# First gate made inside the attention, modulation spread over the MLP, fc2 sums in fc1's PSUM banks, relu squared on ScalarE

## The chip, the cores and the metric

The kernel runs on one core of a Trainium2 chip. The metric is the device time of one execution in microseconds; the time before is the median of three runs.

## The reference, cut to what matters

Two trunk layers work on 128 context tokens and 512 latent tokens, 1024 wide, all in float32. A conditioning vector (one for the context, one for the latents) gives six modulation vectors per layer: shift, scale and gate for the attention, shift, scale and gate for the MLP.

```python
def modulation(cond, w_ada_l, b_ada_l):
    m = (silu(cond) @ w_ada_l + b_ada_l)[:, None, :]
    return split(m, 6)          # vectors 0 to 5
def mlp_residual(x, shift, scale, gate, g, w1, w2):
    h = rms_norm(x, g) * (1 + scale) + shift
    return x + gate * (square(relu(h @ w1)) @ w2)
for l in range(2):
    h = rms_norm(y, norm_mix_g[l]) * (1 + m[1]) + m[0]
    o = diff_attend(h) if l == 0 else neighbourhood_attend(h)
    y = y + m[2] * (o @ w_o[l])          # m[2]: the first gate
    y = mlp_residual(y, m[3], m[4], m[5], norm_mlp_g[l], w_fc1[l], w_fc2[l])
```

`w_fc1` is 1024 by 4096, `w_fc2` 4096 by 1024, `w_ada` 1024 by 6144 per layer.

## The kernel before, in words

The 640 tokens are five tiles of 128. Every float32 product is three matmuls on a high and a low part (`hi`, `lo`): `split` makes the high part with a ScalarE copy and the low part with a subtraction on VectorE (or GpSimd). Weights come in column chunks of 384, 256 and 384 (`CHUNKS`); `load_block` loads one into three `raw` buffers and splits it into one of two `w` buffers. All loads are issued by SyncE (SP), whose queue runs in order.

Layer 0's attention goes over 8 groups of heads times 5 token tiles in slots; `SLOT` and `START` are orders written out by hand (`pin` holds PE, VectorE, ScalarE and GpSimd to them). A digit stands for so many projection matmuls; `fma` is one step of `ada_cols`, which makes modulation vectors 4 and 3 of layer 0: two steps of four small matmuls (`ada_products`) for 256 columns, a ScalarE copy, and a step that turns the row into columns (`to_cols`). The steps run in slots with `n < self.FMA`, and what is left is run at once where the tail begins (`begin`). The tail is the output projection `out_proj`; it runs in the last slots at `TAIL` steps per unit, and makes the first gate (vector 2) itself: `gate_steps` calls `ada_rows` three times, each with three loads into the `raw` buffers, eight program matmuls, a copy, and two matmuls that spread the row over 128 partitions. In layer 1 the gate is read from the DRAM tensor `gate_d`.

The MLP goes over `D_FF` in four quarters: `fc1` (8 units of 128 hidden columns, 48 matmuls each, sums in the two double banks tagged `s`) and then `fc2` (three chunks times five token tiles, 24 matmuls each, sums in the two banks tagged `g`). The hidden columns `u` are kept as `hi` and `lo` in nine buffers. `add_gated` multiplies a sum by the gate into a buffer tagged `B` (three of them, shared with `relu`) and adds it to `x`.

In layer 0's MLP `ada_fma` runs beside this (`fill`): 112 units, each a load of 128 rows of `w_ada` (`fraw`, `ahead` + 1 buffers), a multiply-add on VectorE (L427), a scaled copy on ScalarE (L429) and an addition on GpSimd (L430). They make the second gate of layer 0 (16 units) and the six vectors of layer 1. Eight units make one half vector; `finish` (four steps into the next) turns it with 8 transposes (L394) or sums it with matmuls against ones (L405). There is one step at the start, one a unit, and one at the end: 114. Three steps run after each unit of `fc1`, one after each tile of `fc2`. Instructions of the MLP are ordered by the framework's list scheduler, not by hand. The last chunk of the last quarter is `last_chunk`, which also makes the next norm.

Of the kernel before, what the change touches and what calls it, by code (L numbers as in the profile page):

```python
# [15 lines left out]
P = 128  # L16
# [12 lines left out]
LAMBDA_INIT = 0.2  # L29


class Kernel:
# [274 lines left out]
    def ada_rows(self, l, c0, n):  # L307

        nc = self.nc
        view = self.I["w_ada"][l].rearrange("(k p) n -> p k n", p=P)  # L310
        cuts = ((0, 3), (3, 6), (6, 8))
        raws = [self.load_raw(view[:, k0:k1, c0 : c0 + n]) for k0, k1 in cuts]
        pr = self.psum_g(n)
        yield pr
        raws = [raw[:, k] for (k0, k1), raw in zip(cuts, raws) for k in range(k1 - k0)]
        for h in range(2):
            self.ada_products(pr, raws[4 * h : 4 * h + 4], h)
            for _ in range(6):
                yield

# [21 lines left out]
    def ada_cols(self, jobs, pool, ahead):  # L342

        nc = self.nc
        units = [(*job, c0, kh) for job in jobs for c0 in range(0, D, 256) for kh in range(2)]
        raws = []

        def load():
            if len(raws) < len(units):
                l, vec, c0, kh = units[len(raws)]  # L350
                raw = pool.tile([P, 4, 256], F32, tag="fraw", bufs=ahead, name="fraw")
                src = self.I["w_ada"][l, kh * 512 : kh * 512 + 512, vec * D + c0 : vec * D + c0 + 256]
                nc.sync.dma_start(raw, src.rearrange("(k p) n -> p k n", p=P))
                raws.append(raw)

        for _ in range(ahead):
            load()
        yield
        for i, (l, vec, c0, kh) in enumerate(units):
            if kh == 0:  # L360
                pr = self.psum_t().rearrange("p a b -> p (a b)")[:, 0:256]
            self.ada_products(pr, [raws[i][:, k] for k in range(4)], kh)
            load()
            if kh == 1:
                rows = pool.tile([P, 256], F32, tag="ftmp", bufs=2, name="rows")
                nc.scalar.activation(rows, pr, AF.Copy)
                yield
                self.to_cols(l, vec, c0, 256, rows)
            yield

    def ada_fma(self, jobs, pool, ahead, gate=None, share=False, wait=()):
# [15 lines left out]
        def finish(l, vec, h, acc):  # L387
# [19 lines left out]
            for j in range(4):  # L407
                dst = self.gate_d[vec // 3, j // 2 : j // 2 + 1, h * 512 + j % 2 * 256 : h * 512 + j % 2 * 256 + 256]
                nc.sync.dma_start(dst, row[32 * j : 32 * j + 1])
            if l == 0 and h == 1:  # L410
                self.load_gate(1, gate)
# [27 lines left out]
    def load_gate(self, which, gate):  # L439
        for ci in range(2):  # L440
            self.nc.sync.dma_start(gate[ci], self.gate_d[which, ci : ci + 1].partition_broadcast(P))
# [537 lines left out]
    def gate_steps(self, l, c, gate):  # L979
# [3 lines left out]
        if l:  # L983
            for ci in range(2):
                nc.sync.dma_start(gate[ci][:, :n], self.gate_d[0, ci : ci + 1, c0 : c0 + n].partition_broadcast(P))
            yield
            return
        for ci in range(2):
            nc.sync.dma_start(gate[ci][:, :n], self.I["b_ada"][l : l + 1, 2 * D + c0 : 2 * D + c0 + n].partition_broadcast(P))
        rows = self.ada_rows(l, 2 * D + c0, n)  # L990
        pr = next(rows)
        yield
        for _ in rows:
            yield
        row = self.tmp()[:, :n]
        nc.scalar.activation(row, pr, AF.Copy)
        for ci in range(2):
            pb = self.psum_g(n)
            nc.tensor.matmul(pb, self.sel[:, 2 + ci * P : 2 + (ci + 1) * P], row, start=True, stop=True)
            nc.vector.tensor_tensor(gate[ci][:, :n], pb, gate[ci][:, :n], ALU.add)  # L1000
            for _ in range(4):
                yield
# [66 lines left out]
    def fc1(self, l, q, up, fill, w=None, begin=None):  # L1069
# [17 lines left out]
        for c0, n in CHUNKS:  # L1087
# [9 lines left out]
            for i, cs in enumerate(cols):  # L1097
# [9 lines left out]
                nc.scalar.activation(u[:, 0], r, AF.Square)  # L1107
                nc.vector.tensor_tensor(r, r, r, ALU.mult)  # L1108
                nc.vector.tensor_tensor(u[:, 1], r, u[:, 0].bitcast(F32), ALU.subtract)  # L1109
                us.append(u)  # L1110
                for _ in range(3):
                    next(fill, None)
        return us

    def fc2(self, l, q, us, gate, fill, chunks=CHUNKS):
        act = lambda kt, t: (us[kt][:, 0, t * P : (t + 1) * P], us[kt][:, 1, t * P : (t + 1) * P])
        for c0, n in chunks:
            ww = self.load_block(self.I["w_fc2"][l], q * D, c0, n)
# [26 lines left out]
    FMA = 0  # L1145
# [12 lines left out]
    TAIL = 3.75, 2.75  # L1158
    WLO = (0, 1, 2), (0, 1, 2)
    KB, VB, QTB, EB, ATB, UB = 2, (15, 17), 6, 4, (2, 3), 9  # L1160

    def run(self):
# [3 lines left out]
        with ExitStack() as ctx:  # L1166
# [5 lines left out]
            self.gate_d = self.dram.tile([2, 2, D], F32, name="gate_d")  # L1172
# [20 lines left out]
            for l in range(2):  # L1193
# [53 lines left out]
                def early():  # L1247
# [6 lines left out]
                    if l:  # L1254
                        self.load_gate(1, gate)
                        return iter(())
# [3 lines left out]
                    cmF.append(self.ada_fma(jobs, fpool, 2, gate))  # L1260
# [3 lines left out]
                f = iter(()) if l else cmF[1]  # L1264
# [4 lines left out]
                for _ in f:  # L1269
# [80 lines left out]
```

## Time and profile before

| | |
|---|---|
| median of three runs (lowest to highest) | 1797.42 us (1795.93 to 1798.04) |
| profiled execution: time, span | 1797.07 us, 1795.3 us |
| PE, PEld busy | 1708.6 us (95%), 1624.1 us (90%) |
| VectorE (DVE), ScalarE (ACT), GpSimd (POOL) busy | 1133.0 (63%), 836.1 (47%), 527.8 us (29%) |
| mean granted clock of TensorE | 0.982 |
| layer 0's MLP from its first unconditional stretch of `fc1` to its last `fc1` | 472.97 to 860.65 us |
| the same stretch of layer 1's MLP | 1347.90 to 1678.50 us |

Busy times of PE are modelled at their ends, so that "PE busy" tells less than the time from one stretch's start to the next. The two stretches in the last rows hold the same matmuls of `fc1` and `fc2`; layer 1's has no `ada_fma` beside it. A wait is put down to the engine and line that ended it.

### The profile page before, as it was taken

How to read it: one execution, taken by the hardware profiler on the slowest of the kernel's cores; microseconds unless marked ns; L12 is line 12 of the kernel's file. 1: busy time of each engine (PE TensorE's matmuls, PEld its weight loads, DVE VectorE, ACT ScalarE, POOL GpSimd, SP SyncE). 2: the span in 40 equal slices, each digit the busy share in tenths (PEclk: the TensorE clock that was granted, in tenths of full speed). 3: DMA queues.
4: the chain of work that ended last, by engine and by line, in shares of the span. 5: the costliest groups of instructions: out<-in, count | busy, mean ns of one | idle time of the engine just before them, and what ended most of it. 6: DMA issues, size and time to landing. Idle time of an engine off the chain costs nothing.

```text
span 1795.3 us, 30528 instructions
## 1 busy us (share of the span) xinstructions
PE 1708.6 (95%) x11353; PEld 1624.1 (90%) x11353; DVE 1133.0 (63%) x2269; ACT 836.1 (47%) x2426; POOL 527.8 (29%) x575
## 2 busy tenths in 40 slices
PE   7899999998988989979999999999989999999999
PEld 4699999787878989969999899998889999999999
DVE  5588888765888798786345666667673433434343
ACT  4477777643653353441225777777353222132220
POOL 1334444124554353340004654543350000000000
PEclk8899999999999999989999999999999999999999
DMA  9832453432355355343212433332232222222231
GB/s 297 246 92 58 107 135 99 138 115 82 110 161 185 115 168 173 111 136 118 71 63 76 120 97 85 93 104 88 64 109 68 71 72 82 66 88 71 65 98 50
DMA packets 209397, 195.10 MB, mean 109 GB/s; under 512 B 39447, under 2 KB 193087, under 8 KB 209247
## 3 DMA queue, kind: packets, MB, share of 16 engines
q1 hardware_dynamic: 209246, 193.14, 36.2%
q8 instruction: 89, 1.46, 0.3%
q14 instruction: 62, 0.50, 0.1%
HBM read 182.95 MB, written 16.44 MB: 111 GB/s over the span
## 4 chain that ended last, share of the span: by engine, by line
PE 69%; DVE 10%; ACT 8%; DMA 5%; issue 5%; POOL 2%; SPq 1%; DVEq 0%; POOLq 0%; ACTq 0%
PE ps_g L146 40%; PE pz L1081 16%; DMA fraw<-in_w_ada 3%; DVE acc L427 3%; PE ps_t L712 2%; PE ps_t L886 2%; PE ps_t L741 1%; PE ps_s L736 1%; PE ps_s L735 1%; DVE w L42 1%; PE ps_t L875 1%; DVE relu L1108 1%; ACT E L785 1%; ACT sq L631 1%; POOL rs L118 1%
## 5 line engine op out<-in xcount | busy, mean ns | idle before, releaser
L146 PE MATMUL ps_g<-w,hT 128*128 128x384 f32 (+1 forms) x2544 | 538.8, 347 | 12.4 <-ACT hT L41 4.8
L146 PE MATMUL ps_g<-w,u 128*128 128x384 f32 (+1 forms) x2880 | 463.2, 321 | 27.6 <-DVE u L1109 17.3
L146 PEld LDWEIGHTS ps_g<-w,u 128*128 128x128 f32 x2880 | 452.9, 190 | 34.5 <-DVE u L1109 20.8
L1081 PE MATMUL pz<-hT,w 128*128 128x320 f32 x3072 | 459.8, 310 | 9.7 <-ACT relu L1106 4.9
L1081 PEld LDWEIGHTS pz<-hT,w 128*128 128x128 f32 x3072 | 452.6, 188 | 13.8 <-ACT relu L1106 5.9
L146 PEld LDWEIGHTS ps_g<-w,hT 128*128 128x128 f32 x2544 | 425.3, 191 | 24.7 <-ACT hT L41 7.0
L41 ACT ACTIVATE w<-raw 128x1152 fp32r<-128x1152 f32 (+2 forms) x162 | 148.3, 956 | 239.3 <-PE ps_g L146 231.0
L42 DVE TENSOR_TENSOR w<-raw,w 128x1152 fp32r<-128x1152 f32 (+1 forms) x150 | 178.4, 1208 | 90.0 <-ACT w L41 89.7
L972 DVE TENSOR_TENSOR tmp<-ps_g,gate 128x384 f32<-128x384 f32 (+1 forms) x170 | 85.9, 506 | 210.3 <-PE ps_g L146 208.5
L430 POOL TENSOR_TENSOR acc<-acc,ftmp 128x512 f32<-128x512 f32 x98 | 154.6, 1577 | 190.9 <-ACT acc L425 95.0
L107 POOL TENSOR_TENSOR w<-raw,w 128x256 fp32r<-128x256 f32 x184 | 143.1, 797 | 211.2 <-ACT w L103 210.2
L118 POOL TENSOR_TENSOR rs<-var,mhalf 128x4 f32<-128x4 f32 (+1 forms) x120 | 103.1, 862 | 233.1 <-DVE var L117 231.9
L429 ACT ACTIVATE ftmp<-fraw,silu 128x512 f32<-128x512 f32 x98 | 70.4, 723 | 162.4 <-DMA fraw<-in_w_ada 125.1
L1108 DVE TENSOR_TENSOR relu<-relu 128x640 f32<-128x640 f32 x64 | 64.9, 1014 | 112.7 <-ACT u L1107 112.7
L1106 ACT ACTIVATE relu<-pz 128x640 f32<-128x640 f32 x64 | 44.6, 697 | 190.5 <-PE pz L1081 190.4
L427 DVE SCALAR_TENSOR_TENSOR acc<-fraw,silu,acc 128x512 f32<-128x512 f32 x98 | 111.7, 1140 | 7.7 <-DMA fraw<-in_w_ada 6.6
L638 ACT ACTIVATE rawh<-ps_g,rs 128x64 f32<-128x64 f32 x304 | 70.7, 323 | 40.2 <-POOL rs L118 40.2
L973 DVE TENSOR_TENSOR x<-x,tmp 128x384 f32<-128x384 f32 (+1 forms) x130 | 82.9, 638 | 3.8
L735 PE MATMUL ps_s<-kT,qT 128*128 128x320 f32 (+3 forms) x256 | 76.3, 309 | 0.0
L736 PE MATMUL ps_s<-kT,qT 128*128 128x320 f32 (+3 forms) x256 | 76.0, 301 | 0.0
L631 ACT ACTIVATE sq<-ps_g 128x64 f32<-128x64 f32 x304 | 68.2, 224 | 7.2
L860 DVE CUSTOM_DVE_ANT_0 ps_s<-ps_s,bias 128x384 f32<-128x384 f32 x64 | 36.1, 566 | 43.9 <-PE ps_s L736 33.7
(186 smaller groups left out, 2080.4 us busy)
## 6 DMA issues: line engine op xcount, KB each, us to landing
raw<-in_w_fc SPq DMA_DIRECT2D x64, 576.0 KB
fraw<-in_w_ada SPq DMA_DIRECT2D x112, 256.0 KB
raw<-in_w_fc SPq DMA_DIRECT2D x64, 384.0 KB
raw<-in_w_qkv_diff SPq DMA_DIRECT2D x24, 512.0 KB
raw<-in_w_qkv_na SPq DMA_DIRECT2D x24, 512.0 KB
fraw<-in_w_ada SPq DMA_DIRECT2D x16, 512.0 KB
bias<-ball SPq DMA_DIRECT2D x64, 128.0 KB
araw<-in_w_ada SPq DMA_DIRECT2D x8, 768.0 KB
```

The costliest lines, as they stand in the source:

```text
L41: self.nc.scalar.activation(hi, src, AF.Copy)
L42: (eng or self.nc.vector).tensor_tensor(lo, src, hi.bitcast(F32), ALU.subtract)
L107: self.nc.gpsimd.tensor_tensor(lo[:, ks], raws[i][:, ks], hi[:, ks].bitcast(F32), ALU.subtract)
L118: nc.gpsimd.tensor_tensor(out, v[:, :n], self.mhalf[:, :n], ALU.pow)
L146: self.nc.tensor.matmul(ps, a, b, start=first and kt == k0 and i == 0, stop=last and kt == k1 - 1 and i == 2)
L427: nc.vector.scalar_tensor_tensor(acc[:, 0], raw, s[0], acc[:, 0], ALU.mult, ALU.add)
L430: (nc.vector if share and kt % 3 == 2 else nc.gpsimd).tensor_tensor(acc[:, 1], acc[:, 1], tmp, ALU.add)
L631: nc.scalar.activation(sq, ps[:, u * 64 : u * 64 + 64], AF.Square, accum_out=ss[:, u : u + 1])
L735: self.nc.tensor.matmul(out, q[:, 0, u], k, start=True, stop=False)
L736: self.nc.tensor.matmul(out, q[:, 1, u], k, start=False, stop=True)
L972: nc.vector.tensor_tensor(tmp, ps, g, ALU.mult)
L1081: nc.tensor.matmul(pz[:, s, 0:HALF], wp[:, cs], self.hT[:, b, kt, s * HALF : (s + 1) * HALF], start=first and kt == 0, stop=last and kt == ...
```

## The change

- Layer 0's first gate (vector 2) becomes a third job of `ada_cols` in the attention. A row is summed over its two halves by a matmul with `sel`, added to `b_ada` on VectorE and stored in `gate_d` by SP, 256 columns at a time; `gate_steps` then only loads from `gate_d`, in both layers. `FMA` goes from 0 to 7, `TAIL` of layer 0 from 3.75 to 3.1. `ada_rows` is gone; `gate_d` has a row for each layer.
- A `Paced` object hands out the steps of `ada_fma`: 24 over the first `fc1`, as before, and the rest evenly over 3.3 quarters; `ahead` goes from 2 to 4.
- `fc2` sums the token tiles 0 and 1, then 2 and 3, in a double bank tagged `s`, tile 4 in one tagged `g`. In the first chunk the products of `u`'s last two columns for tiles 0 and 1 come after the other products of both tiles.
- In layer 0's `fc2` the addition to `x` moves to GpSimd (but for the last chunk).
- `fc1` squares in place on ScalarE and uses `split`: ScalarE does relu, square and copy, VectorE one subtraction. `u` has eight buffers.

```diff
+class Paced:
+    def __init__(self, steps, first, rest, span):
+        self.steps, self.first, self.rate, self.done, self.taken = steps, first, rest / span, 0.0, 0
+    def go(self, share):
+        self.done += share
+        due = min(self.done * 2, 1.0) * self.first + max(self.done - 0.5, 0.0) * self.rate
+        while self.taken < int(due + 1e-6):
+            self.taken += 1
+            next(self.steps, None)
...
     def ada_cols(self, jobs, pool, ahead):
...
-                self.to_cols(l, vec, c0, 256, rows)
+                if vec % 3 < 2:
+                    self.to_cols(l, vec, c0, 256, rows)
+                else:
+                    pb = self.psum_t().rearrange("p a b -> p (a b)")[0:2, 0:256]
+                    nc.tensor.matmul(pb, self.sel[:, 0:2], rows, start=True, stop=True)
+                    cs = slice(vec * D + c0, vec * D + c0 + 256)
+                    row = pool.tile([2, 256], F32, tag="grow", bufs=2, name="grow")
+                    nc.sync.dma_start(row, self.I["b_ada"][l : l + 1, cs].partition_broadcast(2))
+                    nc.vector.tensor_tensor(row, pb, row, ALU.add)
+                    nc.sync.dma_start(self.gate_d[l, vec // 3, :, c0 : c0 + 256], row)
...
     def gate_steps(self, l, c, gate):
...
-        rows = self.ada_rows(l, 2 * D + c0, n)
-        pr = next(rows)
-        yield
-        for _ in rows:
-            yield
-        row = self.tmp()[:, :n]
-        nc.scalar.activation(row, pr, AF.Copy)
-        for ci in range(2):
-            pb = self.psum_g(n)
-            nc.tensor.matmul(pb, self.sel[:, 2 + ci * P : 2 + (ci + 1) * P], row, start=True, stop=True)
-            nc.vector.tensor_tensor(gate[ci][:, :n], pb, gate[ci][:, :n], ALU.add)
-            for _ in range(4):
-                yield
+            nc.sync.dma_start(gate[ci][:, :n], self.gate_d[l, 0, ci : ci + 1, c0 : c0 + n].partition_broadcast(P))
+        yield
...
                 nc.scalar.activation(r.rearrange("p (s x) -> p s x", s=2), pz[:, :, 0:HALF], AF.Relu)
-                nc.scalar.activation(u[:, 0], r, AF.Square)
-                nc.vector.tensor_tensor(r, r, r, ALU.mult)
-                nc.vector.tensor_tensor(u[:, 1], r, u[:, 0].bitcast(F32), ALU.subtract)
+                nc.scalar.activation(r, r, AF.Square)
+                self.split(u[:, 0], u[:, 1], r)
                 us.append(u)
-                for _ in range(3):
-                    next(fill, None)
+                fill.go(1 / 16)
...
-            for t in range(NT):
-                self.add_gated(self.x[t], self.product(act, t, ww, n), gate, t, c0, n, c0)
-                if l and q == 3:
-                    self.store(t, c0, n)
-                next(fill, None)
+            for ts in ((0, 1), (2, 3), (4,)):
+                if len(ts) == 2:
+                    pair = self.psum.tile([P, 2, 512], F32, tag="s", bufs=self.PS, name="ps_g")
+                    ps = [pair[:, i, :n] for i in range(2)]
+                else:
+                    ps = [self.psum_g(n)]
+                late = KT - 2 if c0 == 0 and ts[0] == 0 else KT
+                for i, t in enumerate(ts):
+                    for _ in self.product_steps(ps[i], act, t, ww, 0, late, last=late == KT):
+                        pass
+                for i, t in enumerate(ts):
+                    if late < KT:
+                        for _ in self.product_steps(ps[i], act, t, ww, late, KT, first=False):
+                            pass
+                    self.add_gated(self.x[t], ps[i], gate, t, c0, n, c0, None if l else self.nc.gpsimd)
+                    if l and q == 3:
+                        self.store(t, c0, n)
+                    fill.go(n / D / NT / 2)
...
-    FMA = 0
+    FMA = 7
...
-    TAIL = 3.75, 2.75
+    TAIL = 3.1, 2.75
...
-    KB, VB, QTB, EB, ATB, UB = 2, (15, 17), 6, 4, (2, 3), 9
+    KB, VB, QTB, EB, ATB, UB = 2, (15, 17), 6, 4, (2, 3), 8
...
-                    fma = self.ada_cols([(0, 4), (0, 3)], fpool, 4)
+                    fma = self.ada_cols([(0, 4), (0, 3), (0, 2)], fpool, 4)
...
-                    cmF.append(self.ada_fma(jobs, fpool, 2, gate))
+                    cmF.append(Paced(self.ada_fma(jobs, fpool, 4, gate), 24, 8 * len(jobs) - 21, 3.3))
```

## Rows read from the trace of the kernel before

**Rows 1.** Windows of both MLPs: length; PE, PEld, DVE, ACT, POOL busy; clock; DMA.

```profile
472.97:860.65 387.68, 353.86 (x2297) 344.93 (x2298) 308.15 (x345) 154.30 (x211) 155.68 (x99) 0.96 0.46 142
1347.90:1678.50 330.60, 330.59 (x2183) 329.63 (x2184) 136.07 (x187) 78.52 (x99) 1.12 (x1) 1.00 0.23 72
```

**Rows 2.** Layer 0: first two fc2 passes, third fc1, third fc2; same columns.

```profile
527.34:600.01 72.67, 62.56 (x385) 60.07 (x385) 55.53 (x75) 24.53 (x33) 25.47 (x18) 0.93 0.49 155
662.70:727.39 64.69, 60.15 (x386) 58.31 (x385) 49.85 (x61) 22.73 (x31) 23.13 (x15) 0.97 0.47 145
727.39:786.31 58.92, 58.92 (x412) 58.90 (x410) 51.33 (x60) 28.11 (x40) 25.45 (x17) 1.00 0.51 157
786.31:860.65 74.34, 61.45 (x382) 59.00 (x381) 47.70 (x59) 18.54 (x25) 17.17 (x12) 0.91 0.31 96
```

**Rows 3.** Waits of PE in layer 0's MLP: total us, times, longest.

```profile
PE ps_g L146 <- DVE u L1109: 17.3, 5, 5.3
PE ps_g L146 <- ACT u L1107: 7.4, 2, 4.1
PE pz L1081 <- ACT relu L1106: 4.9, 3, 2.7
```

**Rows 4.** Timeline of PE, first change from fc1 to fc2: start, length, [idle before].

```profile
527.91 3.44 PE L146 MATMUL ps_g<-w,u 128*128 128x384 f32 x18
534.65 0.62 PE L146 MATMUL ps_g<-w,u 128*128 128x384 f32 x2 [3.30 <-ACT u L1107]
...
541.78 21.93 PE L146 MATMUL ps_g<-w,u 128*128 128x384 f32 x121 [4.08 <-DVE u L1109]
```

**Rows 5.** Timeline of ACT at the same place.

```profile
530.43 0.72 ACT L429 ACTIVATE ftmp<-fraw,silu 128x512 f32<-128x512 f32 x1 [3.17 <-DMA fraw<-in_w_ada]
```

**Rows 6.** Waits of ACT and POOL in layer 0's MLP.

```profile
ACT ftmp L429 <- DMA fraw<-in_w_ada: 125.1, 53, 7.3
POOL acc L430 <- ACT acc L425: 95.0, 11, 16.5
```

**Rows 7.** Waits of SP's queue in layer 0's MLP.

```profile
SPq L384 <- DVE acc L427: 130.6, 86, 5.9
SPq L61 <- DVE w L42: 59.7, 25, 8.6
```

**Rows 8.** Groups by shape, layer 0's MLP: busy us, mean ns, idle before.

```profile
L430 POOL TENSOR_TENSOR acc<-acc,ftmp 128x512 f32<-128x512 f32 x98 | 154.6, 1577 | 190.9 <-ACT acc L425 95.0 <-ACT ftmp L429 90.5 <-DVE acc L427 2.4
...
L427 DVE SCALAR_TENSOR_TENSOR acc<-fraw,silu,acc 128x512 f32<-128x512 f32 x98 | 111.7, 1140 | 7.7 <-DMA fraw<-in_w_ada 6.6
...
L1108 DVE TENSOR_TENSOR relu<-relu 128x640 f32<-128x640 f32 x24 | 32.0, 1333 | 19.8 <-ACT u L1107 19.8
...
L973 DVE TENSOR_TENSOR x<-x,tmp 128x384 f32<-128x384 f32 x29 | 19.7, 681 | 0.7
...
L394 PE MATMUL ps_t<-ident,acc 128*128 128x128 f32 x64 | 8.5, 273 | 0.0
...
L405 PE MATMUL ps_g<-acc,ones 128*32 128x256 f32 x48 | 3.8, 391 | 0.0
```

**Rows 9.** Groups by shape, layer 1's MLP.

```profile
L1108 DVE TENSOR_TENSOR relu<-relu 128x640 f32<-128x640 f32 x24 | 19.8, 823 | 54.5 <-ACT u L1107 54.5
```

**Rows 10.** Groups by line, whole span.

```profile
L973 POOL TENSOR_TENSOR x<-x,tmp 128x384 f32<-128x384 f32 (+1 forms) x40 | 39.0, 981 | 69.4 <-DVE tmp L972 69.3
...
L305 PE MATMUL ps_g<-raw,cond 128*32 128x384 f32 (+1 forms) x48 | 5.1, 458 | 1.6 <-DMA raw<-in_w_ada 1.6
...
L999 PE MATMUL ps_g<-tmp,sel 128*128 128x384 f32 (+1 forms) x12 | 5.7, 575 | 1.6 <-ACT tmp L996 1.6
```

**Rows 11.** Chain of waits at the tail of layer 0's attention: start, us, what.

```profile
349.99 6.59 DMA raw<-in_w_ada
```

**Rows 12.** Window inside layer 0's attention, columns as in rows 1.

```profile
117.00:165.00 48.00, 48.00 (x321) 45.30 (x320) 40.49 (x121) 34.65 (x144) 19.54 (x26) 1.00 0.30 76
```

**Rows 13.** Timeline of PE early in layer 0's attention.

```profile
78.99 1.07 PE L305 MATMUL ps_t<-fraw,cond 128*32 128x256 f32 x16
```

More of the change, by code (lines that the diff above doesn't have):

```diff
@@ L305, in ada_products @@
             self.nc.tensor.matmul(pr[32 * j : 32 * j + 32], self.cond[:, 4 * h + j], w, start=h == 0, stop=h == 1)
[L307 to L318, printed above, removed]
-                yield
     def cols_out(self, l, vec, k0, n, pv):
@@ L407, in finish @@
             for j in range(4):
-                dst = self.gate_d[vec // 3, j // 2 : j // 2 + 1, h * 512 + j % 2 * 256 : h * 512 + j % 2 * 256 + 256]
+                dst = self.gate_d[l, vec // 3, j // 2 : j // 2 + 1, h * 512 + j % 2 * 256 : h * 512 + j % 2 * 256 + 256]
                 nc.sync.dma_start(dst, row[32 * j : 32 * j + 1])
             if l == 0 and h == 1:
-                self.load_gate(1, gate)
+                self.load_gate(0, gate)
         for _ in range(ahead):
@@ L437, in ada_fma, with load_gate @@
         yield
-    def load_gate(self, which, gate):
+    def load_gate(self, l, gate):
         for ci in range(2):
-            self.nc.sync.dma_start(gate[ci], self.gate_d[which, ci : ci + 1].partition_broadcast(P))
+            self.nc.sync.dma_start(gate[ci], self.gate_d[l, 1, ci : ci + 1].partition_broadcast(P))
     def norm(self, x, t, ab):
@@ L982, in gate_steps @@
         c0, n = CHUNKS[c]
-        if l:
-            for ci in range(2):
-                nc.sync.dma_start(gate[ci][:, :n], self.gate_d[0, ci : ci + 1, c0 : c0 + n].partition_broadcast(P))
-            yield
-            return
         for ci in range(2):
-            nc.sync.dma_start(gate[ci][:, :n], self.I["b_ada"][l : l + 1, 2 * D + c0 : 2 * D + c0 + n].partition_broadcast(P))
-        rows = self.ada_rows(l, 2 * D + c0, n)
-        pr = next(rows)
+            nc.sync.dma_start(gate[ci][:, :n], self.gate_d[l, 0, ci : ci + 1, c0 : c0 + n].partition_broadcast(P))
         yield
-        for _ in rows:
-            yield
-        row = self.tmp()[:, :n]
-        nc.scalar.activation(row, pr, AF.Copy)
-        for ci in range(2):
-            pb = self.psum_g(n)
-            nc.tensor.matmul(pb, self.sel[:, 2 + ci * P : 2 + (ci + 1) * P], row, start=True, stop=True)
-            nc.vector.tensor_tensor(gate[ci][:, :n], pb, gate[ci][:, :n], ALU.add)
-            for _ in range(4):
-                yield
     def o_part(self, c, t, k0, k1, gate):
@@ L1171, in run @@
             self.ball = self.dram.tile([6, ROWS, 8, 16, 256], F32, name="ball")
-            self.gate_d = self.dram.tile([2, 2, D], F32, name="gate_d")
+            self.gate_d = self.dram.tile([2, 2, 2, D], F32, name="gate_d")
             self.w_o = [self.I["w_o_diff"][0], self.I["w_o_na"][0]]
@@ L1255, in early @@
                         self.load_gate(1, gate)
-                        return iter(())
+                        return Paced(iter(()), 0, 0, 1)
                     cmF[0], fpool = open_pool("fm", "left")
                     jobs = [(v, vec, h) for v, vec in ((0, 5), (1, 1), (1, 0), (1, 2), (1, 4), (1, 3), (1, 5)) for h in range(2)]
-                    cmF.append(self.ada_fma(jobs, fpool, 2, gate))
+                    cmF.append(Paced(self.ada_fma(jobs, fpool, 4, gate), 24, 8 * len(jobs) - 21, 3.3))
                     return cmF[1]
                 us = self.fc1(l, 0, up, None, w1[0], early)
-                f = iter(()) if l else cmF[1]
+                f = Paced(iter(()), 0, 0, 1) if l else cmF[1]
                 for q in range(4):
@@ L1268, in run @@
                     self.fc2(l, q, us, gate, f, CHUNKS if q < 3 else CHUNKS[:2])
-                for _ in f:
+                for _ in f.steps:
                     pass
```

## The prediction

> **What bounds the kernel now.** I read the windows first and set layer 0's MLP against layer 1's. The two stretches hold the same matmuls; layer 1 takes 330.60 us and PE is busy in all of it, layer 0 takes 387.68 and PE is busy for 353.86 [rows 1]. So layer 0's MLP loses 57.1 us, and as only `ada_fma` differs, that is where to look. 33.8 us of it are PE's idle time (387.68 − 353.86). Of the rest, `ada_fma`'s own transposes and sums on PE are 8.5 + 3.8 = 12.3 us of busy time [rows 8]; ends of matmuls overlap, so I take 11. What remains, 57.1 − 33.8 − 11 = 12.3, is clock: the granted clock of the stretch is 0.96, and 0.93, 0.97 and 0.91 in the three fc2 passes [rows 2], so in part of each TensorE ran at the lower of its two levels, 1.2 in place of 2.4 GHz; the third fc1 pass, in which PE was never idle, has 1.00. So 46 of the 57 us can go and 11 stay.
>
> Next, the waits. PE waits most for `u`: 17.3 us for its low part, 7.4 for its high part; in fc1 it waits 4.9 us for relu to free a bank [rows 3]. The timeline shows where: fc2's first tile runs 18 matmuls (six of the eight `u`), and then waits 3.30 and later 4.08 us for the last two [rows 4]. Why is `u` late? ACT runs in order, and there it stood 3.17 us in front of a `ftmp` copy whose `fraw` had not landed, with the relu queued behind it [rows 5]. This is the commonest wait of the stage: ACT waits 125.1 us in 53 places for `fraw` [rows 6]. And `fraw` is late because SP issues its load only when VectorE has let go of one of three buffers, 130.6 us of waiting in 86 places [rows 7]. A pass of fc1 or fc2 without this is 56.3 us (layer 1's 330.60 by 5.87, its first fc1 being counted from the 51st of 384 matmuls), a unit of fc1 an eighth, 7.04 us. A load is issued two steps ahead, and with 3 steps a unit that is some 4.7 us before its use.
>
> **The change part by part.**
>
> *Pace and distance.* Before, a quarter takes 8 × 3 + 15 = 39 steps, so that 114 are gone in 2.9 quarters and the last has none. After, 24 fall in the first fc1, then 91 / 3.3 = 27.6 a quarter, 13.8 a pass of 56.3 us, one each 4.1 us; they end in the second chunk of the last fc2, ahead of the norms that read the vectors. Four steps ahead is then 16 us of lead where it was under 5. SP's queue also waits for `raw` buffers, up to 8.6 us at a time [rows 7], with `fraw` loads behind; 16 us covers that, 5 did not.
>
> *VectorE and GpSimd.* In the three-quarter stretch VectorE loses the multiplication, 32.0 us in 24 instructions, and additions to `x`, 19.7 us for the wide ones alone, and (111.7 us spread over 3.8 quarters, not 3) some 24 us of multiply-adds [rows 8]: 308 − 76 = 232 of about 345 us, 67% where it was 79%. GpSimd gains 55 additions over four quarters at the 0.98 us that it takes for the same operation in the output projection [rows 10], 44 us for the 45 in the stretch, and gives 33 of its 156 away by the pace: 167 us, 48%. A new wait comes with it: an addition to `x` stands in GpSimd's queue among `ada_fma`'s, and three `B` buffers are held until it is done. It costs nothing while VectorE has buffers; the price without that cover is under the rivals.
>
> *ScalarE.* 8 copies more a quarter, at 0.72 us for 512 columns [rows 5], at most 0.9 for 640: 6 to 7 us a quarter on an engine that is busy 154 of 388 us [rows 1]. The way to the last `u` is relu, square, copy, subtract where it was relu, square, multiply, subtract. Hidden behind fc2's first products; with no cover it is some tenths of a us at each of eight changes, 0 to 3 us.
>
> *Order in fc2.* 36 matmuls now stand before the last two `u`, not 18. Eighteen took 3.44 us as recorded [rows 4], so PE has some 3.1 us more (by starts) at each change from fc1 to fc2, and with five sums in flight, not two, a late VectorE stops PE later. In layer 1 PE has no gap to fill [rows 1], so there this, the copy and the eighth buffer bring 0; the buffer's next writer comes after its last reader on PE anyhow. I allow 1 us either way.
>
> *What stays.* The first fc1 keeps its 3 steps a unit; I keep half of fc1's waits, 3 us, and 1 us for each of the three changes from fc1 to fc2: 6 us. From below it is 2, from above 20 (half the waits and the clock with them). MLP: 46 − 6 = 40 us gained.
>
> *First gate.* In the tail go 48 recorded matmuls of `ada_products`, 5.1 us busy, and 12 of `sel`, 5.7, with 1.6 us of idle time before each [rows 10]: 14.0 us, of which I take 12, as ends overlap. There go with it nine loads through `raw` (the chain has one of 6.59 us in it [rows 11], with the weights of the output projection behind it on SP), three copies and six additions. TAIL shrinks with the number of steps, so the real work stays in its slots. In the attention come eight units: 8 loads of 512 KB, 4 copies, 4 additions, 8 small DMAs, and on PE four times 16 recorded matmuls at 1.07 us [rows 13] and four `sel` products, which the trace does not have; nearest is `sel` in the tail, 575 ns per recorded matmul [rows 10], two thirds as wide here, so 8 × 0.38 = 3.1 us. Sum 7.4, I take 7, and all of it counts, since PE is busy 48.00 of 48 us there [rows 12]. The store waits on SP for VectorE's addition, with `fraw` and projection weights behind it; SP moves 76 GB/s there, and the loads are issued tens of us early, so nothing is charged. Between bounds: 14 − 4 = 10 us gained, or 3 − 9 = 6 lost; I take 12 − 7 = 5 gained.
>
> **The sum.** 40 + 5 = 45 us. The profiled execution took 1797.07 us (span 1795.3), the median of the runs is 1797.42: 0.35 apart, so 1752 us on either.
>
> **The rivals.**
>
> *SP's queue holds `fraw` back, not the distance.* If `raw` waits (59.7 us [rows 7]) come in a row, 16 us of lead are used up and ACT stands as before; only the order in fc2 helps. Then the changes keep their stalls less 3.1 us each, about 15 of 25 us, and half the clock loss and fc1's waits, 11 more: 46 − 26 = 20 gained, with the gate 25: 1772 us. Against it: the longest is 8.6 us. 15%.
>
> *GpSimd takes from VectorE what it gives.* The multiplication takes 1333 ns in layer 0 and 823 in layer 1, where GpSimd is idle [rows 8, 9]: the two slow each other. Their records add to 308 + 156 = 464 us in 388, 1.20 times the time. After, 232 + 167 = 399; at 1.20 that needs 332 us, just under PE's 342 (330.6 + 11). If additions to `x` overlap worse, at 1.10, it is 363: 21 us back, of which my 6 are a part, so 1752 + 15 = 1767. Against it: the third fc1 pass shows 51.33 + 25.45 in 58.92, 1.30 times, without one idle moment of PE [rows 2]. 10%. The Trainium skill speaks for this rival (SBUF — State Buffer, section "Who interferes with whom"): a VectorE instruction with two SBUF inputs and a GpSimd one that reads SBUF exclude each other, the later waiting for the earlier to end; the trace agrees on the slowing, 823 to 1333 ns.
>
> *Slower: GpSimd's queue ties fc2 to `ada_fma`.* GpSimd waits 95.0 us in 11 places for the first copy of a half vector, up to 16.5 us [rows 6]. Before, nothing of fc2 stood behind; now additions to `x` do. Three buffers and three to five sums are some 20 us of cover, so I expect none to reach PE. It decides once more than 45 us come through, half of these waits; all would give 1752 + 95 = 1847 us. 4%.
>
> *No change*: MLP gain eaten by new waits in the last quarter, which was free of `ada_fma`: 1797. 2%.
>
> **How the numbers follow.** My forecast has 69%, with a range of its own of 1740 to 1762 (6 us of rest from 2 to 12, the gate between its bounds). Faster by over 0.2% (3.6 us, about what can be told here): 69 + 15 + 10 = 94%; the same 2%; slower 4%. The range of 8 in 10 reaches from 1738, everything at its good bound, to 1776, the first rival with a little more.
>
> **What would show it.** The stretch of layer 0's MLP at 345 to 350 us with a clock of 0.99 or more; no wait of PE for `u` over 2 us; ACT's wait for `fraw` below 40 us; layer 1's passes at 56.3 us as now; the fma slots of the attention about 1 us longer each, the tail 10 us shorter. Wrong is the argument if ACT still stands for `fraw`, or if PE waits for `tmp` behind GpSimd.

## The result and the profile after

After the change the kernel takes 1767.24 us (median of four runs, 1765.76 to 1769.35); the kernel before took 1797.71 us beside it. The ratio is 0.9833, 95% interval 0.9816 to 0.985: 30 us faster, where 45 were forecast. The profiled execution has a span of 1767.6 us, 27.7 less than the one before (1795.3). One run of the last kernel below, 2079.20 us at a granted clock of 0.75, lies far above the five others of that kernel and is left out of its row. In the changed kernel the products of `fc1` are line L1076, those of `fc2` L160, `split` is L55 (ScalarE) and L56 (VectorE), `add_gated` L984 (multiply) and L985 (add), `ada_fma` L439, L441 and L442, its finishes L406 and L417.

The windows of layer 0's MLP, columns as in [rows 1]: the three-quarter stretch, then the first `fc2`, the third `fc1` and the third `fc2`, as in [rows 2].

```profile
473.26:832.46 359.20, 343.25 (x2262) 338.57 (x2263) 248.24 (x251) 160.71 (x221) 188.11 (x129) 0.98 0.47 145
526.98:593.12 66.14, 59.53 (x368) 58.89 (x369) 42.56 (x48) 23.06 (x31) 35.60 (x28) 0.95 0.49 155
709.40:767.27 57.87, 57.87 (x402) 57.26 (x401) 26.81 (x27) 30.89 (x43) 19.32 (x13) 1.00 0.41 123
767.27:832.46 65.19, 59.15 (x371) 58.83 (x370) 45.16 (x52) 20.30 (x28) 38.52 (x28) 0.95 0.42 130
```

The stretch is 359.20 us where it was 387.68 and where 345 to 350 were forecast. The first and third `fc2` pass take 66 and 65 us at a clock of 0.95; the `fc1` between them has 57.87, a clock of 1.00 and no idle moment. So most of what is missing is in two passes. The waits of this MLP (us in total, times, longest), for [rows 3] and [rows 6]:

```profile
ACT ftmp L441 <- DMA fraw<-in_w_ada: 21.0, 11, 7.0
...
PE ps_g L160 <- DVE tmp L984: 14.1, 4, 6.0
...
PE ps_g L160 <- DVE u L56: 0.9, 1, 0.9
```

What the forecast set out to cure is cured: ACT's wait for `fraw` fell from 125.1 us to 21.0, PE's for `u` from 24.7 us to 0.9. Another has grown: PE waits 14.1 us for the multiplication by the gate, where before it was

```profile
PE ps_g L146 <- DVE tmp L972: 2.8, 3, 1.3
```

The timeline of PE at the first change from `fc1` to `fc2`, for [rows 4]:

```profile
526.98 7.43 PE L160 MATMUL ps_g<-w,u 128*128 128x384 f32 x41 [0.15 <-ACT relu L1101]
535.30 1.50 PE L160 MATMUL ps_g<-w,u 128*128 128x384 f32 x7 [0.89 <-DVE u L56]
542.51 17.74 PE L160 MATMUL ps_g<-w,u 128*128 128x384 f32 x99 [5.71 <-DVE tmp L984]
```

48 matmuls run, with 0.89 us of waiting for the last `u`. Then PE stands for 5.71 us, though weights and `u` are all there. VectorE in that time:

```profile
534.43 0.81 DVE L56 TENSOR_TENSOR u<-relu,u 128x640 fp32r<-128x640 f32 x1
535.17 1.77 DVE L439 SCALAR_TENSOR_TENSOR acc<-fraw,silu,acc 128x512 f32<-128x512 f32 x1
536.86 3.68 DVE L56 TENSOR_TENSOR w<-raw,w 128x768 fp32r<-128x768 f32 x2
540.46 1.53 DVE L439 SCALAR_TENSOR_TENSOR acc<-fraw,silu,acc 128x512 f32<-128x512 f32 x2
541.90 0.55 DVE L984 TENSOR_TENSOR tmp<-ps_g,gate 128x384 f32<-128x384 f32 x1
```

VectorE does the next weights' subtractions and three multiply-adds first, and PE goes on 0.06 us after tile 0's multiplication has ended (541.90 + 0.55). What was PE about to run? No view of the profile shows that, but the program that is built from the kernel does. PE's part of its instruction list, from the last product of tile 0 (`ps_g_6994` is the double bank of tiles 0 and 1, `ps_g_7060` that of tiles 2 and 3; DVE_49 and PE_49 are the semaphores that VectorE and PE count up):

```
L160 MATMUL ps_g_6994<-w_6981,u_6941 128x384 [waits DVE_49]
L160 MATMUL ps_g_7060<-w_6981,u_6415 128x384 [waits PE_49]
L160 MATMUL ps_g_7060<-w_6981,u_6415 128x384 x2
L160 MATMUL ps_g_7060<-w_6981,u_6464 128x384 x3
L160 MATMUL ps_g_6994<-w_6981,u_6868 128x384 [waits DVE_49]
```

The seven matmuls at 535.30 are the first four of these rows. The one that stands is the last row, the first late product of tile 1, and it waits for VectorE: in the program, until the instruction has ended that multiplies tile 0's sum by the gate. It needs nothing of that instruction's: all its operands were ready by 535.24 (534.43 + 0.81). But `fc2` issues tile 0's multiplication before tile 1's late products, and both tiles' sums lie in one buffer.

The stall costs more than its length. The windows after it, columns as in [rows 1]:

```profile
536.80:542.51 5.71, 0.00 (x0) 0.00 (x1) 5.67 (x7) 1.78 (x3) 3.11 (x2) 0.74 0.38 118
...
542.51:544.00 1.49, 1.49 (x5) 1.49 (x6) 0.60 (x1) 0.00 (x0) 1.47 (x2) 0.50 0.82 231
544.00:545.50 1.50, 1.50 (x6) 1.50 (x5) 0.66 (x2) 0.25 (x1) 1.24 (x2) 0.50 0.90 226
545.50:547.00 1.50, 1.50 (x8) 1.50 (x8) 0.56 (x1) 0.47 (x1) 1.50 (x2) 0.73 1.04 365
```

After 5.71 us without a matmul the granted clock is 0.50, TensorE's lower level (1.2 GHz), for the 3 us of the second and third row, where 11 matmuls start; in the next 1.5 us 8 start, and from 547 us on the clock is 1.00.

### The profile page after: what moved, and what is told of

Read it like the earlier page. It is cut to its first block, busy times and chain, and to the rows that moved or that the text cites. A ratio compares the mean times of both kernels' runs of the same rounds, so it can differ in the third digit from the quotient of the medians.

```text
span 1767.6 us, 30599 instructions
## 1 busy us (share of the span) xinstructions
PE 1696.0 (96%) x11365; PEld 1617.8 (92%) x11365; DVE 1059.5 (60%) x2148; ACT 881.7 (50%) x2491; POOL 591.5 (33%) x630
## 4 chain that ended last, share of the span: by engine, by line
PE 77%; ACT 7%; DVE 6%; POOL 3%; issue 3%; DMA 3%; SPq 1%; DVEq 0%; POOLq 0%; ACTq 0%
PE ps_g L160 43%; PE pz L1076 21%; PE ps_t L724 2%; PE ps_t L898 2%; PE ps_t L753 1%; PE ps_s L748 1%; PE ps_s L747 1%; PE ps_t L887 1%; DVE acc L439 1%; POOL acc L442 1%; ACT E L797 1%; POOL rs L132 1%; ACT sq L643 1%; ACT rawh L650 1%; ACT hf L480 1%
## 5 line engine op out<-in xcount | busy, mean ns | idle before, releaser
L160 PE MATMUL ps_g<-w,hT 128*128 128x384 f32 (+1 forms) x2544 | 541.5, 348 | 11.3 <-DVE tmp L984 4.8
L160 PE MATMUL ps_g<-w,u 128*128 128x384 f32 (+1 forms) x2880 | 455.0, 319 | 13.9 <-DVE tmp L984 12.7
L160 PEld LDWEIGHTS ps_g<-w,u 128*128 128x128 f32 x2880 | 448.0, 189 | 17.8 <-DVE tmp L984 12.7
L1076 PE MATMUL pz<-hT,w 128*128 128x320 f32 x3072 | 457.9, 310 | 5.6 <-ACT hT L55 2.5
L1076 PEld LDWEIGHTS pz<-hT,w 128*128 128x128 f32 x3072 | 451.1, 188 | 9.4 <-ACT hT L55 3.6
L160 PEld LDWEIGHTS ps_g<-w,hT 128*128 128x128 f32 x2544 | 426.4, 192 | 24.3 <-ACT hT L55 6.3
L55 ACT ACTIVATE w<-raw 128x1152 fp32r<-128x1152 f32 (+1 forms) x162 | 150.2, 955 | 218.3 <-PE ps_g L160 204.9
L56 DVE TENSOR_TENSOR w<-raw,w 128x1152 fp32r<-128x1152 f32 (+1 forms) x150 | 183.0, 1243 | 103.8 <-ACT w L55 103.6
L984 DVE TENSOR_TENSOR tmp<-ps_g,gate 128x384 f32<-128x384 f32 (+1 forms) x170 | 82.8, 505 | 223.2 <-PE ps_g L160 219.8
L442 POOL TENSOR_TENSOR acc<-acc,ftmp 128x512 f32<-128x512 f32 x98 | 164.5, 1679 | 131.5 <-ACT acc L437 103.7
L985 POOL TENSOR_TENSOR x<-x,tmp 128x384 f32<-128x384 f32 (+1 forms) x95 | 94.0, 1002 | 165.7 <-DVE tmp L984 165.0
L56 DVE TENSOR_TENSOR u<-relu,u 128x640 fp32r<-128x640 f32 x64 | 63.6, 994 | 117.6 <-ACT u L55 117.5
L441 ACT ACTIVATE ftmp<-fraw,silu 128x512 f32<-128x512 f32 x98 | 70.8, 723 | 118.4 <-POOL acc L442 96.0
L439 DVE SCALAR_TENSOR_TENSOR acc<-fraw,silu,acc 128x512 f32<-128x512 f32 x98 | 127.3, 1299 | 2.7 <-DMA fraw<-in_w_ada 0.4
```

Of the source, the lines that this page charges most:

```text
L55: self.nc.scalar.activation(hi, src, AF.Copy)
L56: (eng or self.nc.vector).tensor_tensor(lo, src, hi.bitcast(F32), ALU.subtract)
L160: self.nc.tensor.matmul(ps, a, b, start=first and kt == k0 and i == 0, stop=last and kt == k1 - 1 and i == 2)
L439: nc.vector.scalar_tensor_tensor(acc[:, 0], raw, s[0], acc[:, 0], ALU.mult, ALU.add)
L442: (nc.vector if share and kt % 3 == 2 else nc.gpsimd).tensor_tensor(acc[:, 1], acc[:, 1], tmp, ALU.add)
L985: (eng or nc.vector).tensor_tensor(x[:, c0 : c0 + n], x[:, c0 : c0 + n], tmp, ALU.add)
```

## The experiments

Twelve kernels, each timed in five rounds. The intervals are about 0.2% wide to each side, 3.6 us. The run of the kernel before that stood beside them had medians of 1797.81 us (first four), 1796.44 (next four) and 1800.96 (last four); where the two differ, the ratio is the better measure. The first row is the change itself.

| kernel | us, median (lowest to highest) | ratio to before, 95% |
|---|---|---|
| the change | 1767.24 (1765.76 to 1769.35) | 0.9833 (0.9816 to 0.985) |
| the change, additions apart | 1752.11 (1749.72 to 1753.22) | 0.9747 (0.9729 to 0.9765) |
| the change, gate in the tail | 1771.60 (1767.48 to 1773.90) | 0.9860 (0.9842 to 0.9878) |
| the change, old order of fc2 | 1780.87 (1779.95 to 1782.08) | 0.9910 (0.9895 to 0.9924) |
| the change, x on VectorE | 1770.30 (1768.84 to 1770.71) | 0.9848 (0.9831 to 0.9866) |
| apart, old square | 1759.58 (1757.03 to 1760.85) | 0.9794 (0.9774 to 0.9815) |
| apart, two steps ahead | 1754.52 (1752.41 to 1756.30) | 0.9770 (0.9748 to 0.9793) |
| apart, gate in the tail | 1753.89 (1753.33 to 1754.60) | 0.9764 (0.9742 to 0.9787) |
| apart, old pace | 1766.76 (1766.39 to 1767.10) | 0.9836 (0.9814 to 0.9858) |
| apart, x on VectorE | 1753.68 (1750.05 to 1755.62) | 0.9745 (0.9722 to 0.9769) |
| apart, TAIL 3.75 | 1757.08 (1753.59 to 1759.35) | 0.9765 (0.9742 to 0.9788) |
| before, with the order alone | 1779.26 (1777.68 to 1784.79) | 0.9901 (0.9876 to 0.9926) |
| before, with pace and distance alone | 1787.56 (1783.93 to 1790.37) | 0.9935 (0.9911 to 0.9959) |

**The additions apart.** One loop is cut in two, so that both tiles' late products are issued before either sum is read.

```diff
                 for i, t in enumerate(ts):
                     if late < KT:
                         for _ in self.product_steps(ps[i], act, t, ww, late, KT, first=False):
                             pass
+                for i, t in enumerate(ts):
                     self.add_gated(...)
```

> The change as it is, but the additions to x of token tiles 0 and 1 come after the late products of both, so that no read of the double bank stands between the two tiles' products. Theory, shared bank: the two sums are one buffer to the framework, and the late products of tile 1 wait until VectorE has read tile 0's sum; the profile of the changed kernel has PE waiting 14.1 us in 4 places for that multiplication (5.7 and 6.0 us at the first and third change to fc2), and a granted clock of 0.95 in those two passes. Without the wait the two passes go from 66.1 and 65.2 us to 58 to 59, the clock back to 1.00: 1767 - 14 = 1753 us (1750 to 1757). Rival, VectorE late: VectorE is late with its sums as such (weights' subtractions and multiply-adds stand ahead of them), and PE stops a little later for the next bank: 1762 to 1768 us.

1752.11 us, 15 less than the change. The windows of the stretch and of the two passes, then the timelines of PE and VectorE at the same place as above:

```profile
472.65:815.89 343.24, 339.12 (x2262) 335.25 (x2263) 249.90 (x251) 160.72 (x221) 187.61 (x129) 1.00 0.48 152
526.39:584.79 58.40, 57.59 (x369) 57.27 (x369) 43.71 (x48) 23.08 (x31) 35.62 (x28) 1.00 0.54 175
758.80:815.89 57.09, 57.09 (x371) 57.09 (x370) 45.76 (x52) 20.28 (x28) 38.02 (x28) 1.00 0.46 148
```

```profile
526.39 7.51 PE L160 MATMUL ps_g<-w,u 128*128 128x384 f32 x41 [0.18 <-ACT relu L1101]
534.70 14.47 PE L160 MATMUL ps_g<-w,u 128*128 128x384 f32 x81 [0.81 <-DVE u L56]
```

```profile
536.27 3.75 DVE L56 TENSOR_TENSOR w<-raw,w 128x768 fp32r<-128x768 f32 x2
539.94 1.53 DVE L439 SCALAR_TENSOR_TENSOR acc<-fraw,silu,acc 128x512 f32<-128x512 f32 x2
541.38 1.01 DVE L984 TENSOR_TENSOR tmp<-ps_g,gate 128x384 f32<-128x384 f32 x2
```

VectorE multiplies no earlier than before, at 541.38, which is 15.0 us after the pass begins (541.90 and 14.9 in the change), after the same subtractions and multiply-adds, but PE runs through. So the stall was the shared buffer and not a late VectorE: the rival is out. Of the 14.1 us of waits the two long ones are gone and 2.4 us stay:

```profile
PE ps_g L160 <- DVE tmp L984: 2.4, 2, 1.5
```

The two passes lose 66.14 − 58.40 = 7.74 and 65.19 − 57.09 = 8.10 us, together 15.8: the waits of 5.71 and 6.0 us and the low clock behind them. The stretch is 343.24 us at a clock of 1.00.

**The first gate back in the tail**, on the change and on the version with the additions apart.

```diff
-    FMA = 7
+    FMA = 0
-    TAIL = 3.1, 2.75
+    TAIL = 3.75, 2.75
-   fma = self.ada_cols([(0, 4), (0, 3), (0, 2)], fpool, 4)
+   fma = self.ada_cols([(0, 4), (0, 3)], fpool, 4)
+   # gate_steps makes the gate with ada_rows for l == 0, as before
```

> The change without its first part: layer 0's first gate is made in the tail, as before. Theory, the gate moved for nothing: layer 0's first fc1 starts at 461.44 us before and 461.73 after, because the attention became 8.6 us longer and the tail only some 8.5 shorter: VectorE's chain sets the tail's slots, and the time that the gate's matmuls leave becomes waits for it. Then 1767 us, within 2. Rival, the forecast: the move is worth 5 us, hidden by something else that the trace compares badly, and this kernel takes 1772 us (1770 to 1774).

> With the sums' additions apart as the base (1752.11 us), the first gate of layer 0 is made in the tail as before. Theory, moved for nothing: the profile of the same undoing without the base shows layer 0's first fc1 at 461.83 us, against 461.73 with the gate moved and 461.44 before: 1752 us, within 2. Rival, the forecast of 5 us: 1757 us (the medians of the two earlier kernels, 1771.60 and 1767.24, are 4.4 apart, with overlapping intervals).

The medians say 4.4 and 1.8 us for the move, the ratios 5 and 3; the intervals overlap in both pairs, though the second pair's runs lie just apart (1753.33 and up against 1753.22 and down). By the time alone the first of the two runs came out as the rival had it, and not within 2 us of 1767. The traces are the sharper tool, since the move ends where layer 0's first `fc1` begins: in the five profiles with the gate in the tail that is at 461.44, 461.83, 462.51, 460.84 and 462.46 us (mean 461.82), in the eight with the gate moved and TAIL at 3.1 at 461.73, 461.11, 461.84, 462.07, 462.17, 461.13, 459.83 and 461.43 (mean 461.41). The move is worth 0.4 us by these, less than the 1.7 and 2.3 us by which each group spreads, and at most a few by the runs.

**The old order and banks of fc2.**

```diff
-            for ts in ((0, 1), (2, 3), (4,)):
-                ... (double bank, late products, additions)
+            for t in range(NT):
+                self.add_gated(self.x[t], self.product(act, t, ww, n), gate, t, c0, n, c0, None if l else self.nc.gpsimd)
```

> The change with the old fc2: one sum after another in the two banks tagged g, all 24 products of a tile in a row; additions to x stay on GpSimd. Theory, shared bank: the 14.1 us of waits for the multiplication go, and the waits for the last u come back: its low part is there 8.3, 5.0, 6.2 and 5.9 us after fc2 begins, and is wanted 4.0 us after it, so about 4, 1, 2 and 2 us. In layer 1, where fc2 takes 56.3 us a pass before and 55.5 after without any wait, the passes go back to 56.3 if the banks make that: 3 us. Together 1767 - 14 + 9 + 3 = 1765 us (1760 to 1770). Rival, the order itself is the gain (the forecast gave it 3.1 us at each change): 1779 us or more, with waits for u as long as before.

1780.87 us, 14 more than the change and 29 more than the version with the additions apart; the rival's number (1779 or more) holds and mine does not, though the waits for `u` are not as long as before (24.7 us [rows 3]). Its waits in layer 0's MLP:

```profile
PE ps_g L160 <- DVE tmp L984: 11.1, 9, 3.9
PE ps_g L160 <- DVE u L56: 4.8, 2, 2.8
PE ps_g L160 <- ACT ftmp L441: 3.3, 1, 3.3
PE ps_g L160 <- ACT u L55: 2.5, 3, 1.4
```

I had counted the waits for `u`; what I left out stands in the first row: with two single banks PE waits nine times for a late multiplication anywhere in a pass. As I read it, the double banks save these 11.1 us and the order the 10.6 of the other rows; no run has the one without the other.

**The additions to x on VectorE**, on both versions (the last argument of `add_gated` goes).

> The change with the additions to x of layer 0's fc2 back on VectorE. Theory: VectorE has 30 to 60% idle time in the passes, so 55 additions of 0.6 to 0.7 us hide; the multiplication of tile 0 is late as before. 1767 us, within 4. Rival, GpSimd takes from VectorE what it gives: additions on GpSimd slow VectorE by sharing its way to memory, and taking them back shortens the first and third fc2 pass by several us: under 1762 us.

> With the sums' additions apart as the base (1752.11 us), the additions to x of layer 0's fc2 go back to VectorE. Theory: what the additions cost VectorE shows only where PE waits for it; without the base that was 3 us (1770.30 against 1767.24), with 16.0 us of waits for tmp in place of 14.1. On the base these waits are 2.4 us, so 1752 to 1755 us. Rival, GpSimd takes from VectorE what it gives: with GpSimd relieved of 45 us of additions VectorE's own instructions shorten, 1748 us or less.

3 us slower on the change, with overlapping intervals, where the false wait grows (16.0 us), and 1.6 or nothing with the additions apart: where PE does not wait for VectorE, relieving VectorE brings nothing. In the profiles layer 0's MLP alone takes 492.83 us with the additions to `x` on VectorE against 491.06 on the change, and 473.47 against 475.35 with the sums' additions apart: there the move to GpSimd gained nothing. The groups by shape, first of the version with the additions apart (x on GpSimd), then with x on VectorE:

```profile
L439 DVE SCALAR_TENSOR_TENSOR acc<-fraw,silu,acc 128x512 f32<-128x512 f32 x84 | 108.0, 1286 | 2.5 <-DMA fraw<-in_w_ada 0.3 <-DVE acc L439 0.3
...
L985 POOL TENSOR_TENSOR x<-x,tmp 128x384 f32<-128x384 f32 x29 | 31.0, 1091 | 43.6 <-DVE tmp L984 43.6
```

```profile
L439 DVE SCALAR_TENSOR_TENSOR acc<-fraw,silu,acc 128x512 f32<-128x512 f32 x84 | 103.9, 1237 | 3.2 <-DMA fraw<-in_w_ada 1.1 <-DVE acc L439 0.3
...
L985 DVE TENSOR_TENSOR x<-x,tmp 128x384 f32<-128x384 f32 x29 | 17.4, 629 | 0.1
```

GpSimd does take something back: the multiply-adds take 1286 ns with the additions on GpSimd and 1237 without, 4 us over 84. VectorE's busy time in the stretch goes from 266.33 to 249.90 us, so that of 24 us taken off it (17.4 + 6.3 for the narrow ones) 16.4 stay off.

The Trainium skill's rule (SBUF — State Buffer, "Who interferes with whom"), that such instructions of the two engines exclude each other, agrees with this slowing in its direction. How strictly they exclude each other no run here shows; the two engines' records add to 249.9 + 187.6 us in 343.2.

**The old square** (ScalarE squares into `u`'s high part, VectorE multiplies again).

```diff
-                nc.scalar.activation(r, r, AF.Square)
-                self.split(u[:, 0], u[:, 1], r)
+                nc.scalar.activation(u[:, 0], r, AF.Square)
+                nc.vector.tensor_tensor(r, r, r, ALU.mult)
+                nc.vector.tensor_tensor(u[:, 1], r, u[:, 0].bitcast(F32), ALU.subtract)
```

> With the sums' additions apart (1752.11 us) as the base, the square goes back to the old way: ScalarE squares into the high part, VectorE multiplies again and subtracts. Theory, VectorE's load matters: 32 multiplications of 0.8 to 1.3 us stand again in its queue before the last u of each fc1, some 1.0 to 1.3 us at each of four changes, and the waits for u and for tmp grow: 1756 to 1760 us. Rival, hidden: the forecast's cover (36 products ahead of the last two u) takes it in: 1752 us, within 2. A side question: layer 1's fc2 passes take 56.3 us before and 55.5 after; if the square makes that, they go back to 56.3 (3 us in all).

1759.58 us: 7.5 more, the theory's number. Its mechanism is shown in part only: in the profile layer 0's MLP is 479.78 us long, against 475.35 with the square on ScalarE, and 2.85 of these 4.4 us are in the first `fc1` pass; PE's waits for `u` are 1.5 us (0.8 with the square on ScalarE) and for `tmp` 1.8 (2.4). Another 3.2 us are in layer 1's attention (940.91 to 1314.27 us, against 936.46 to 1306.62), which has no square; the other profiles have 369.0 to 373.3 us there, so these 3.2 are hardly the square's. The side question is answered too: layer 1's passes do not go back to 56.3 us, so the square does not make their difference.

**Two steps ahead, and the old pace.** Two kernels, each with one of the two undone.

```diff
-   cmF.append(Paced(self.ada_fma(jobs, fpool, 4, gate), ...))
+   cmF.append(Paced(self.ada_fma(jobs, fpool, 2, gate), ...))
...
-        self.done += share
-        due = min(self.done * 2, 1.0) * self.first + max(self.done - 0.5, 0.0) * self.rate
-        while self.taken < int(due + 1e-6): ...
+        for _ in range(3 if share == 1 / 16 else 1):
+            next(self.steps, None)
```

> With the sums' additions apart as the base (1752.11 us), the loads of fraw are issued two steps ahead again, not four, at the new pace (a step each 4.1 us, so 8 us of lead in place of 16). Theory, the distance cures the waits for fraw, as in the forecast: the longest wait of SP's queue was 8.6 us, so ACT's waits for fraw come back in part (from some 20 us to 50 or more) and the time is 1757 to 1762 us. Rival, the pace does it: 8 us are enough: 1752 us, within 2.

> With the sums' additions apart as the base (1752.11 us), the old pace: three steps after each unit of fc1, one after each tile of fc2, and nothing left for the last quarter; the loads stay four steps ahead (9.4 us of lead in fc1). Theory, the pace matters: some 24 us of VectorE's multiply-adds and 33 of GpSimd's additions go back into the first three quarters and crowd each fc1, so the last u is late again: 1757 to 1765 us, with PE waiting over 10 us for u and tmp. Rival, the distance alone: 1752 us, within 2.

The distance is worth 2.4 us by the medians (4 by the ratios, with overlapping intervals), nearer to the rival than to the theory; the pace is worth 14.7 (16), somewhat more than its theory had. With two steps ahead ACT waits for `fraw` more than twice as long as with four (29.9 us with the additions apart), and PE hardly sees it:

```profile
ACT ftmp L441 <- DMA fraw<-in_w_ada: 69.2, 38, 4.9
```

With the old pace and the long distance ACT's wait for `fraw` is 30.4 us, and PE waits all the same, for relu, `u` and weights, and less than expected for `u` and `tmp` (line numbers here are 3 lower):

```profile
PE pz L1073 <- ACT relu L1098: 4.6, 2, 4.4
PE ps_g L157 <- DVE u L53: 4.0, 2, 3.2
PE pz L1073 <- DVE w L53: 2.2, 2, 1.5
```

Layer 0's MLP takes 949.74 − 461.43 = 488.31 us there, 13.0 more than with the new pace. That it is the crowding of each `fc1` I conclude from the second and third `fc1` pass, 65.18 and 61.17 us (58.05 and 57.87).

**TAIL at 3.75 with the gate moved.**

> With the sums' additions apart as the base (1752.11 us), TAIL of layer 0 is 3.75 again, with the gate still made in the attention: each slot of the tail holds a fifth more of the output projection. Theory: PE idles 7.5 us in the tail's slots for VectorE's og because the slots hold too little of PE's work once the gate's matmuls are gone; with more in each slot part of that is filled: 1748 to 1750 us. Rival: the slots only become longer, or other waits take the place: 1752 us, within 2.

1757.08 us, 5 more (3 by the ratios) and above both numbers expected, and the first `fc1` begins at 465.47 us in place of 461.11. Its waits in the tail:

```profile
PE ps_t L764 <- DVE og L828: 9.9, 6, 2.4
PE ps_t L724 <- DVE hT L56: 2.8, 1, 2.8
```

More of PE's work in each slot fills no gap: PE waits longer for both (7.5 and 2.3 us with TAIL at 3.1).

**One part alone on the kernel before**: `fc2` with double banks, late products and the additions apart (and nothing else), and pace with distance (and eight buffers for `u`).

> The kernel before with one part of the change alone: fc2's sums in the double banks and the last terms of two tiles late, with the additions after both (as in the run with the sums' additions apart). Pace, distance, gate, square and additions as before. Theory: the order and the banks are the largest part, as the run with the old order took 28.8 us more than the run with the sums apart (1780.87 against 1752.11): alone some 15 to 30 us: 1768 to 1783 us. Rival, the forecast's account, 3.1 us at each of three or four changes: 1785 to 1789 us.

> The kernel before with one part of the change alone: the steps handed out evenly over 3.3 quarters, the loads four steps ahead, eight buffers for u (nine do not leave the room). Theory of the forecast, that the waits for fraw are the root: they go, and with them most of the 25 us of waits for u and half the clock loss: 1757 to 1768 us. Rival, from the runs so far: undoing the pace cost 14.7 us and the distance 2.4, and with the old order the waits for u and for the two single banks stay: 1778 to 1786 us.

By the ratios the order and banks alone give 18 us (0.9901), pace and distance alone 12 (0.9935); the first is as expected, the second at the upper end of the rival's numbers and far from the theory's. In the second, ACT's wait for `fraw` is 56.6 us and no longer 125.1, but PE's waits are:

```profile
PE ps_g L160 <- DVE tmp L986: 13.4, 7, 3.7
...
PE ps_g L160 <- DVE u L1123: 6.5, 3, 3.9
```

Neither part does it alone. As I read it, VectorE is late in bursts around each change from `fc1` to `fc2`, and it takes both fewer steps in the burst and sums that let PE go on through it.

## Why the prediction was right in sign and 15 us too far

1767.24 us lies inside the range of 8 in 10 (1738 to 1776) and above the forecast's own (1740 to 1762). Neither range follows from the bounds given: they make 1743 to 1769 of the forecast's own and 1742 of everything at its good bound, and the rest of the MLP has 20 as its upper bound in one place and 12 in another. That 1767 is also the second rival's time is chance: its mechanism asks for a gain when the additions to `x` go back to VectorE, and that kernel took 1770.30 us.

*MLP, −40 us: got −24.6.* From the first `fc1` to the next projection layer 0's MLP took 977.06 − 461.44 = 515.62 us before and 952.79 − 461.73 = 491.06 after. The step of the prediction that failed is the sentence on the order in `fc2`, "with five sums in flight, not two, a late VectorE stops PE later". That holds for every pair but one: at the first pair of a pass, where the late products follow, the additions stand between them, and the two sums are then one buffer in which tile 1 waits for tile 0's reader. The diff shows it; I counted banks and did not follow the order of reads and writes in one. With the additions apart the MLP takes 936.46 − 461.11 = 475.35 us, 40.3 less than before, and the kernel 1752.11 us. So the term was worked out for a kernel without this wait, and is right for that one, in part by luck: the stretch came to 343.24 us where 347.7 were counted (387.68 − 40), and `ada_fma`'s new work in the last quarter, for which I had no term, shows: its last quarter takes 936.46 − 815.89 = 120.57 us, against 977.06 − 860.65 = 116.41.

*The root of it, the distance: wrong.* I read ACT's 125.1 us of waits for `fraw` as the cause of the late `u`. The runs show that PE needs them cured only in small part: with 69.2 us of them the kernel takes 1754.52 us, and with 30.4 us of them and the old pace 1766.76. The pace and the banks carry the gain.

*VectorE 232 us in the stretch, GpSimd 167: 248.24 and 188.11.* The multiplications left as counted. The multiply-adds fell only from 98 to 84 in the stretch and each took longer (1264 ns, 1140 before [rows 8]), so 5.6 us went in place of 24.

*SP's queue as the rival had it: no.* Its waits for VectorE to let go of a `raw` buffer even grew in the three-quarter stretch, from 59.7 us [rows 7] to 97.3, and ACT's for `fraw` fell all the same. (The 59.7 us, with 8.6 the longest, are those of the stretch and not of the whole MLP, which has 145.5 us and 17.6; the change has 135.8 there.)

```profile
SPq L75 <- DVE w L56: 97.3, 38, 13.4
```

*PE's waits for `u` under 2 us, ACT's for `fraw` below 40 us: right* (0.9 and 21.0 us). "PE waits for `tmp`" was my sign of a failed argument, but I looked for it behind GpSimd; it was VectorE's queue, and nothing of GpSimd stood in it.

*First gate, −5 us: about 0.* PE's work in the attention was right: 7.4 us worked out, and the groups by line up to the end of the attention show 64 more matmuls with the condition, 4.9 us busy (14.1 − 9.2), and 2.4 us of `sel`. First before, then after:

```profile
L305 PE MATMUL ps_t<-fraw,cond 128*32 128x256 f32 x128 | 9.2, 401 | 1.3 <-DVE qT L718 0.9 <-ACT ot L810 0.4
```

```profile
L319 PE MATMUL ps_t<-fraw,cond 128*32 128x256 f32 x192 | 14.1, 396 | 0.9 <-DVE ab L332 0.9
...
L375 PE MATMUL ps_t<-rows,sel 128*2 128x256 f32 x8 | 2.4, 378 | 0.0
```

The gain in the tail, 12, was too large. PE's waits there, first before, then after:

```profile
PE ps_t L752 <- DVE og L816: 4.3, 4, 2.6
```

```profile
PE ps_t L764 <- DVE og L828: 7.5, 6, 2.3
PE ps_t L724 <- DVE hT L56: 2.3, 1, 2.3
```

The gate's matmuls had 3.2 us of idle time before them [rows 10], and PE now waits 3.2 us more for `og` (a head's output, scaled by its norm on VectorE). What is late next in these slots is `og`, which the sum did not ask. From corresponding slots to the first `fc1` (344.50 to 461.44 us before, 353.50 to 461.73 after) the tail became 8.7 us shorter, with 14.4 us of idle time on PE in both kernels, and the attention before it 9.0 longer, 1.7 more than PE's new work.

*Layer 1, 0 ± 1: 3 us faster.* See below. From layer 0's MLP on the change is 3.4 us shorter; with the MLP's 24.6 and the 0.3 us by which its first `fc1` begins later this makes the 27.7 us between the two profiles.

## What to carry to other kernels

Where two sums share one buffer of the framework's, list its reads and writes in program order before counting it as two: here a read of one half between writes of the other made a wait, and cutting one loop in two took it away (15 us). The longest wait of a trace is not yet the cause; ask what waits behind it and whether PE ever does. And a wait taken out of a slot that another engine sets can come back under that engine's name, as it did in the tail.

## What the runs showed of the hardware that was not expected

A pause of 5.71 us cost PE 7.74: behind it 11 matmuls of 384 columns started in 3 us, at a granted clock of 0.50, where 19 start in the 3 us from 547 us on, at 1.00.

Layer 1's `fc2` passes take several lengths for the same 360 matmuls without one wait on PE. The timelines of PE of before, of the change, and of before with the order alone:

```profile
1396.99 56.45 PE L146 MATMUL ps_g<-w,u 128*128 128x384 f32 x360
```

```profile
1372.43 55.41 PE L160 MATMUL ps_g<-w,u 128*128 128x384 f32 x360
```

```profile
1380.50 55.37 PE L146 MATMUL ps_g<-w,u 128*128 128x384 f32 x360
```

Before, the first three passes took 56.3 us each from start to start; in the change and in the twelve kernels they took 55.2 to 56.1, with the square old or new, the banks old or new, eight buffers for `u` or nine. This is the 3 us of layer 1. What makes it stays open.
